# Two-layer decoder trunk: the next stage opens with token tile 0 alone, weights are split further ahead

## The chip, the cores and the metric

The kernel runs on one core of a Trainium2 chip. The metric is the device time of one execution in microseconds (us); lower is better. The engines are named as the profile names them: PE (TensorE matmul) and PEld (its weight loads), DVE (VectorE), ACT (ScalarE), POOL (GpSimd), SP (SyncE).

## The reference

Batch 1, 256 tokens, width 2048, two layers. All matrix products are in float32.

```python
h = x
for layer in range(2):
    if layer == 0: attn = moba_attention(h, w_qkv, w_o, rel_bias)   # 16 heads of 128; one block of 256 tokens: causal
    else:
        k, v = h @ w_kv                                              # 4 shared K/V heads
        attn = swa_attention(h, w_q, sinks, w_o, k, v, rel_bias)     # 16 query heads, window of 128, a sink per head
    h = layer_norm(ALPHA * h + attn, ln_g[layer, 0], ln_b[layer, 0])
    c = causal_conv_width_3(h @ w_up[layer]) + conv_b                # 2048 -> 2 x 5504
    g, v = split(c)
    ffn = (gelu(g) * v) @ w_down[layer]                              # 5504 -> 2048
    h = layer_norm(ALPHA * h + ffn, ln_g[layer, 1], ln_b[layer, 1])
```

## The kernel before, in words

**Numbers.** A float32 value is kept as the sum of a high part and a low part (`fp32r`). A product is three matmuls: high by high, high weight by low activation, low weight by high activation. The transposed activations lie in the tile `xT` as 16 blocks (`KB`) of 128 features; a block has 512 columns: the high parts of tokens 0 to 255, then their low parts. Token tile 0 is tokens 0 to 127, token tile 1 tokens 128 to 255.

**Weights.** All weights come as one stream of 724 pieces `[128, 1024]`, called halves. SP loads a half (512 KB) into one of four `raw` buffers. `split_upto(i)` emits, for each half up to number i, a copy of the high part by ACT (L86, `wh`) and the subtraction that leaves the low part by DVE (L87, `wl`), and then the load of a further half (L72). There are four places for split halves (`HALF_BUFS`). `take()` gives PE the next half after asking for splits three halves ahead (`AHEAD`). Every engine works through its own instructions in program order; the order is written by hand (`at`, `pe_at`: so many half-steps later).

**Stages.** Attention 0, feed-forward 0 (FFN 0), attention 1, feed-forward 1 (FFN 1). In an up-projection or a q or k projection, one unit (`ws_unit`) is 128 output features: two halves, 16 high-part weight blocks against all 512 columns (L229) and 16 low-part blocks against 256 (L232). In `project_out`, and for v, the weights move instead (L251 to L253): four chunks of 512 output columns, each with one accumulator for each token tile.

**Between stages.** The last 16 blocks (8 halves) of the last chunk of `project_out`, the window, are computed for token tile 0 first and then for token tile 1 (`tilewise`). So the layer norm of tile 0 runs while PE works on tile 1. To hold 8 halves, four of them lie in `xT`, which is idle then (`aside`, `SPARE`). After the norm (L322, L323, one pair for each of four column groups), `turn` transposes four blocks on PE (L332) and copies them into `xT` (ACT, L334), and `low` makes the low parts (DVE, L339). The norm of tile 1 can only start when PE has done the window. Before an FFN, the first unit runs 32 matmuls over the 256 high columns of both tiles (L213, L214), so each block waits for tile 1's turn; its 16 matmuls with the low columns follow (L218). Before attention 1, the v projection does its first 8 blocks for tile 0 alone.

**Pools.** Attention has its own pool (with `oT`, its output) and the FFN has its own (with `aT`, its activations); each opens when its stage begins.

Of the kernel before, what the change touches and what calls it, by code (L numbers as in the profile page):

```python
# [17 lines left out]
P = 128  # L18
# [11 lines left out]
WINDOW = 128  # L30
# [13 lines left out]
WINDOW_BLOCKS = 2 * (HALF_BUFS + SPARE)  # L44


@with_exitstack
def trunk(ctx: ExitStack, tc: tile.TileContext, wst, xT_in, x_in, relb, onehot, umask, sinks, conv_in, ln_g, ln_b, out):
# [13 lines left out]
    todo = {"load": 0, "split": 0}  # L62
# [12 lines left out]
    def split_upto(i):  # L75
        while todo["split"] <= min(i, n_halves - 1):
            s = todo["split"]
            r = raws.pop(s)
            if s in aside:
                j = aside.pop(s)  # L80
                wh, wl = (xT[:, k:k + 2, :].rearrange("p a b -> p (a b)") for k in (4 * j, 4 * j + 2))
            else:
                wh = spool.tile([P, HW], F32R, name="wh")
                wl = spool.tile([P, HW], F32R, name="wl")
            for c in pieces(s):
                nc.scalar.activation(wh[:, c], r[:, c], AF.Copy)  # L86
                nc.vector.tensor_tensor(out=wl[:, c], in0=r[:, c], in1=wh[:, c].bitcast(F32), op=ALU.subtract)  # L87
            halves[s] = (wh, wl)
            todo["split"] += 1
            load_weights()  # L90
# [24 lines left out]
    def take(ahead=AHEAD):  # L115
        i = nexth["i"]
        nexth["i"] += 1
        split_upto(i + ahead)
        run(before)
        return halves.pop(i)  # L120

    xT = big.tile([P, KB, 2 * T], F32R, name="xT")
    res = big.tile([P, 2, D], F32, name="res")

# [75 lines left out]
    def ws_unit(acc, feed=None):  # L200

        def cols(w, j):
            return w[:, j * P:(j + 1) * P]

        o = acc[:, 0:T]
        if feed:
            pair = [take(1 - i) for i in range(2)]
            for k in range(KB):  # L210
                feed(k)
                wh, wl = pair[k // 8]
                nc.tensor.matmul(o, cols(wh, k % 8), xT[:, k, 0:T], start=(k == 0), stop=False)  # L213
                nc.tensor.matmul(o, cols(wl, k % 8), xT[:, k, 0:T], start=False, stop=False)  # L214
            feed(KB)
            split_upto(nexth["i"] + AHEAD - 2)
            for k in range(KB):
                nc.tensor.matmul(o, cols(pair[k // 8][0], k % 8), xT[:, k, T:2 * T], start=False, stop=(k == KB - 1))  # L218
                if k % 8 == 7:
                    step()  # L220
                    split_upto(nexth["i"] + AHEAD - 2 + (k + 1) // 8)
                    if k < 8:
                        run(before)
            return
        for hf in range(2):
            wh, wl = take()
            for j in range(8):
                k = hf * 8 + j
                nc.tensor.matmul(acc, cols(wh, j), xT[:, k, :], start=(k == 0), stop=False)  # L229
            for j in range(8):  # L230
                k = hf * 8 + j
                nc.tensor.matmul(o, cols(wl, j), xT[:, k, 0:T], start=False, stop=(k == KB - 1))  # L232
            step()

    class Moving:
# [12 lines left out]
        def mm(self, acc, k, t, wh, wl):  # L248
            sh = self.src[:, k, t * P:(t + 1) * P]
            sl = self.src[:, k, T + t * P:T + (t + 1) * P]  # L250
# [20 lines left out]
        def chunk(self, accs, early=None, late=None):  # L271
# [3 lines left out]
            if early:  # L275
                k = 2 * HALF_BUFS
                self.tilewise(accs, 0, k, early)
# [14 lines left out]
    def project_out(src, nk, li, after, preload):  # L292
# [4 lines left out]
        aside.update({w0 + j: j for j in range(SPARE)})  # L297
# [44 lines left out]
        pts = {}  # L342

        def late(t, i):
            last = i == WINDOW_BLOCKS // 2 - 1
# [6 lines left out]
            if t == 1 and after and i >= SPARE:  # L352
                c = COLS[0][i - SPARE]
                pts[c] = turn(0, c)
                if not last:
                    low(0, c, pts[c])
                if i < SPARE + 2:
                    split_upto(w0 + WINDOW_BLOCKS // 2 + i - SPARE)
            if t == 1 and last:
                evac(NCH - 1, 1, accs[1])  # L360
                sd = moments(1)
                if after:
                    low(0, c, pts[c])
# [5 lines left out]
        for n in range(NCH):  # L369
            accs = [acc_tile(), acc_tile()]  # L370
            if n < NCH - 1:
# [71 lines left out]
    def layer_attention(l, rest):  # L443
        with tc.tile_pool(name=f"att{l}", bufs=2) as pool:
            oT = pool.tile([P, NH, 2 * T], F32R, name="oT", bufs=1)
            bias = pool.tile([P, NH, 2 * P], F32, name="bias", bufs=1)
            if l == 0:
                load_input(pool, lambda: bias_table(pool))
            else:
                nc.vector.tensor_scalar(nsk, sk, -1.0, None, op0=ALU.mult)  # L450
            for i, h in enumerate(range(0, NH, 4)):
                at(4 + (8 - 4 * l) * i, spread_bias, l, h, h + 4)
                at(4 + (8 - 4 * l) * i, load_bias, bias, l, h, h + 4)

            def v_group(early=None):
                mv = Moving(xT, KB)
                accs = [acc_tile(), acc_tile()]
                mv.chunk(accs, early=early)
                vt = pool.tile([P, 2, 512], F32, name="vt", bufs=1 if l else 2)

                def evac():
                    for t in range(2):
                        nc.scalar.activation(vt[:, t, :], accs[t], AF.Copy)

                at(0, evac)
                return vt

            def feat_unit(name, bufs):
                acc = acc_tile()
                ws_unit(acc)  # L470
                o = pool.tile([P, T], F32, name=name, bufs=bufs)

                def evac():
                    nc.scalar.activation(o, acc[:, T:2 * T], AF.Copy)
                    nc.vector.tensor_tensor(out=o, in0=acc[:, 0:T], in1=o, op=ALU.add)

                at(0, evac, first=True)
                return o

            if l == 0:  # L480
                for g in range(NH // 4):
                    vt = v_group()
                    for j in range(4):
                        h = 4 * g + j
                        q = feat_unit("qT", 4)
                        k = feat_unit("kT", 4)
                        attention(pool, l, h, q, vt[:, :, j * P:(j + 1) * P], k, bias, oT)
            else:
                norm, turned = rest
                for i, c in enumerate(COLS[0][:2]):  # L490
                    split_upto(nexth["i"] + 2 + i)
                    norm(c)

                def early(t, i):
                    if i == HALF_BUFS - 1:
                        turn, low = turned
                        pts = [(c, turn(c)) for c in (COLS[0][2:] if t else COLS[0][:2])]
                        for c, pt in pts:
                            low(c, pt)
                        if t == 0:  # L500
                            for c in COLS[0][2:]:
                                norm(c)
                    if t:
                        split_upto(nexth["i"] + i)

                vt = v_group(early)
                ks = [feat_unit("kT", KVH) for _ in range(KVH)]
                for h in range(NH):
                    q = feat_unit("qT", 4)
                    j = h // GRP  # L510
                    attention(pool, l, h, q, vt[:, :, j * P:(j + 1) * P], ks[j], bias, oT)
            return project_out(oT, NH, 2 * l, True, AF.Gelu_apprx_tanh)

    def layer_ffn(l, rest):
        with tc.tile_pool(name=f"ffn{l}", bufs=2) as pool:
            aT = pool.tile([P, FT, 2 * T], F32R, name="aT", bufs=1)
            cw = pool.tile([P, FT, 2, 4], F32, name="cw", bufs=1)
            nc.gpsimd.dma_start(cw, conv_in[l])
            norm, turned = rest
            turn, low = turned  # L520
            for c in COLS[1]:
                norm(c)
            pts = {}

            def feed(k):
                for b, c in zip(((0, 0),) + COLS[1], COLS[1]):
                    if k == b[0] and c not in pts:
                        pts[c] = turn(c)
                if k == KB:
                    for c in COLS[1]:  # L530
                        low(c, pts[c])

            def conv(i, s, acc, whole, c):
                w = cw[:, i, s, :]
                h = acc[:, 0:T]
                if not whole:
                    h = pool.tile([P, T], F32, name="h")
                    nc.scalar.activation(h, acc[:, T:2 * T], AF.Copy)
                    nc.vector.tensor_tensor(out=h, in0=acc[:, 0:T], in1=h, op=ALU.add)  # L539
# [115 lines left out]
```

## Time and profile before

| | us |
|---|---|
| median of 3 runs (2109.34 to 2110.36) | 2110.07 |
| the profiled execution | 2108.28 |
| its span, first to last instruction | 2106.2 |
| PE busy in the span | 2077.7 |
| DVE busy | 1434.3 |
| ACT busy | 989.6 |

The profile is one execution. A busy PE in it may still be a slow PE, because the ends of matmuls are modelled; the distance from one start to the next is what tells. The mean granted TensorE clock of the run is 0.996 of full speed.

### The profile page before, as it was taken

What the parts mean: (1) busy time and instruction counts of PE and PEld (TensorE: products, weight loads), DVE (VectorE), ACT (ScalarE), POOL (GpSimd) and SP (SyncE); (2) the same over time, 40 slices, a digit from 0 to 9 for tenths busy, and PEclk for the clock granted to TensorE, in tenths of its full rate; (3) what the DMA queues carried; (4) which work ended last, traced back from release to release, by engine and by line L of the source; (5) the groups of instructions that cost most, each with busy time, mean ns of one, the idle gap of its engine ahead of it and who ended that gap; (6) DMA issues with size and microseconds to landing.
All of it is one profiled execution on the core that took longest, in us unless ns stands there. A gap on an engine that the chain in (4) does not pass through costs nothing.

```text
span 2106.2 us, 28530 instructions
## 1 busy us (share of the span) xinstructions
PE 2077.7 (99%) x10972; PEld 1788.4 (85%) x10972; DVE 1434.3 (68%) x2104; ACT 989.6 (47%) x1395; POOL 23.5 (1%) x36
## 2 busy tenths in 40 slices
PE   9999999999999999999999999999999999999997
PEld 7888888788888888888887888888888888888886
DVE  5555555787787787754457676687787778764455
ACT  5454444355545455433344554455555554543342
POOL 0100000000000000000001000000000000000000
PEclk9999999999999999999999999999999999999999
DMA  8854546565555555556566544565555555555563
GB/s 279 293 191 170 178 163 204 180 207 189 187 188 189 190 190 188 185 190 198 193 207 214 212 146 159 180 214 190 190 189 183 191 187 189 190 189 191 193 196 130
DMA packets 114265, 405.08 MB, mean 192 GB/s; under 512 B 15649, under 2 KB 15969, under 8 KB 112849
## 3 DMA queue, kind: packets, MB, share of 16 engines
q1 hardware_dynamic: 106832, 383.67, 54.3%
q0 software_dynamic: 7008, 19.33, 2.6%
q8 instruction: 86, 1.41, 0.3%
q14 instruction: 51, 0.41, 0.1%
q10 hardware_dynamic: 288, 0.26, 0.0%
HBM read 401.02 MB, written 6.34 MB: 193 GB/s over the span
## 4 chain that ended last, share of the span: by engine, by line
PE 97%; DVE 2%; ACT 0%; issue 0%; DMA 0%; ACTq 0%; DVEq 0%
PE acc L229 39%; PE acc L232 20%; PE acc L252 12%; PE acc L251 12%; PE acc L253 12%; PE at L393 1%; PE at L426 1%; DVE wl L87 1%; PE at L419 0%; DVE res L322 0%; PE at L392 0%; PE at L427 0%; DVE res L323 0%; DVE xT L339 0%; PE at L332 0%
## 5 line engine op out<-in xcount | busy, mean ns | idle before, releaser
L87 DVE TENSOR_TENSOR wl<-raw,wh 128x1024 fp32r<-128x1024 f32 (+1 forms) x709 | 865.1, 1222 | 592.2 <-ACT wh L86 589.8
L86 ACT ACTIVATE wh<-raw 128x1024 fp32r<-128x1024 f32 (+1 forms) x709 | 750.3, 1059 | 901.0 <-PE acc L253 341.7
L229 PE MATMUL acc<-xT,wh 128*128 128x512 f32 x3552 | 896.3, 394 | 0.0
L229 PEld LDWEIGHTS acc<-xT,wh 128*128 128x128 f32 x3552 | 640.8, 189 | 116.0
L232 PEld LDWEIGHTS acc<-xT,wl 128*128 128x128 f32 x3552 | 484.5, 190 | 34.8
L232 PE MATMUL acc<-xT,wl 128*128 128x256 f32 x3552 | 495.2, 282 | 0.0
L251 PE MATMUL acc<-wh,aT 128*128 128x512 f32 x656 | 255.5, 389 | 0.0
L252 PE MATMUL acc<-wl,aT 128*128 128x512 f32 x656 | 255.2, 389 | 0.0
L253 PE MATMUL acc<-wh,aT 128*128 128x512 f32 x656 | 255.2, 389 | 0.0
L253 PEld LDWEIGHTS acc<-wh,aT 128*128 128x128 f32 x656 | 123.1, 188 | 25.6
L252 PEld LDWEIGHTS acc<-wl,aT 128*128 128x128 f32 x656 | 123.1, 188 | 25.5
L251 PEld LDWEIGHTS acc<-wh,aT 128*128 128x128 f32 x656 | 123.1, 188 | 25.4
L251 PE MATMUL acc<-wh,oT 128*128 128x512 f32 x224 | 88.9, 397 | 0.0
L253 PE MATMUL acc<-wh,oT 128*128 128x512 f32 x224 | 87.3, 390 | 0.0
L252 PE MATMUL acc<-wl,oT 128*128 128x512 f32 x224 | 87.3, 390 | 0.0
L541 DVE SCALAR_TENSOR_TENSOR c<-h,cw,c 128x255 f32<-128x255 f32 x170 | 82.2, 484 | 6.0
L542 DVE SCALAR_TENSOR_TENSOR c<-h,cw,c 128x254 f32<-128x254 f32 x170 | 82.2, 483 | 6.1
L540 DVE TENSOR_SCALAR c<-h,cw 128x256 f32<-128x256 f32 x170 | 70.1, 412 | 6.1
L539 DVE TENSOR_TENSOR h<-acc,h 128x256 f32<-128x256 f32 x170 | 70.8, 417 | 0.0
L251 PE MATMUL acc<-wh,xT 128*128 128x512 f32 x160 | 65.2, 408 | 4.8 <-ACT wh L86 4.6
L548 ACT ACTIVATE aT<-c 128x256 fp32r<-128x256 f32 x86 | 35.9, 418 | 69.8 <-DVE c L545 69.8
L252 PE MATMUL acc<-wl,xT 128*128 128x512 f32 x160 | 63.5, 397 | 1.7 <-DVE wl L87 1.7
(100 smaller groups left out, 1190.4 us busy)
## 6 DMA issues: line engine op xcount, KB each, us to landing
raw<-in_wst_dram SPq DMA_DIRECT2D x723, 512.0 KB, 3.4
band<-ud POOLq DMA_DIRECT2D x8, 512.0 KB, 14.3
bias<-band POOLq DMA_DIRECT2D x8, 512.0 KB, 5.7
gb<-in_ln_g_dram POOLq DMA_DIRECT2D x4, 1024.0 KB, 6.6
gb<-in_ln_b_dram POOLq DMA_DIRECT2D x4, 1024.0 KB, 9.3
res<-in_x_dram POOLq DMA_DIRECT2D x2, 1024.0 KB, 10.3
out_dram<-res SPq DMA_DIRECT2D x8, 256.0 KB, 2.5
xc<-in_xT_dram SPq DMA_DIRECT2D x7, 256.0 KB, 5.4
```

Source lines behind the costliest of these rows:

```text
L86: nc.scalar.activation(wh[:, c], r[:, c], AF.Copy)
L87: nc.vector.tensor_tensor(out=wl[:, c], in0=r[:, c], in1=wh[:, c].bitcast(F32), op=ALU.subtract)
L229: nc.tensor.matmul(acc, cols(wh, j), xT[:, k, :], start=(k == 0), stop=False)
L232: nc.tensor.matmul(o, cols(wl, j), xT[:, k, 0:T], start=False, stop=(k == KB - 1))
L251: nc.tensor.matmul(acc, sh, wh, start=(k == 0), stop=False)
L252: nc.tensor.matmul(acc, sh, wl, start=False, stop=False)
L253: nc.tensor.matmul(acc, sl, wh, start=False, stop=(k == self.nk - 1))
L539: nc.vector.tensor_tensor(out=h, in0=acc[:, 0:T], in1=h, op=ALU.add)
L540: nc.vector.tensor_scalar(c, h, w[:, 2:3], w[:, 3:4], op0=ALU.mult, op1=ALU.add)
L541: nc.vector.scalar_tensor_tensor(c[:, 1:T], h[:, 0:T - 1], w[:, 1:2], c[:, 1:T], op0=ALU.mult, op1=ALU.add)
L542: nc.vector.scalar_tensor_tensor(c[:, 2:T], h[:, 0:T - 2], w[:, 0:1], c[:, 2:T], op0=ALU.mult, op1=ALU.add)
L548: nc.scalar.activation(aT[:, i, 0:T], g, AF.Copy)
```

## The change

1. **Opening of an FFN.** `ws_opening` replaces the first four ordinary units: 16 high-part blocks of each of four units against the high and low columns of token tile 0 alone (a 2 by 128 pattern of columns, into the same pattern of the accumulator); then the same 64 blocks against tile 1, four blocks of each unit in turn, after the turn of those blocks; then the low parts of the four units as in an ordinary unit.
2. **Opening of attention 1.** The v projection does all 16 blocks for tile 0 and then all 16 for tile 1, before the attention pool opens.
3. **Splitting ahead.** High and low parts are counted apart (`high_upto`, `split_upto`). From the second chunk of a `project_out` on, split halves also lie in idle activations: before an FFN in `xT` (4), in `up` (6) and in the four old places, 14 in all; before attention 1 in `xT` and the four old places, 8, and for the window also in `st` and `up`. `reach` says how far `take` asks ahead. By the end of the window the first eight halves of the next stage have their high parts asked for, the first six also their low parts.
4. **Pools.** `st` is one constant tile for the attention output and the first 16 blocks of the FFN's activations; `up` holds the other 27 and opens after the first chunk of the attention's `project_out` (`turnover`), with the load of `cw`. The pool of attention 1 opens after its v projection, so its bias loads start there.
5. The turns of tile 0 in the window come one half earlier. Line numbers move: L87 is L99 in the changed kernel, L86 L92, L332 L384, L229 L232, L232 L235.

```diff
+    def ws_opening(accs, between, done):
+        n0 = nexth["i"]
+        nexth["i"] += 2 * len(accs)
+        run(before)
+        pair = [[halves.pop(n0 + 2 * u + i) for i in range(2)] for u in range(len(accs))]
+        def high(u, t, ks):
+            part = lambda a: a.rearrange("p (s t c) -> p s t c", s=2, t=2)[:, :, t, :]
+            for k in ks:
+                nc.tensor.matmul(part(accs[u]), cols(pair[u][k // 8][0], k % 8), part(xT[:, k, :]),
+                                 start=(t == 0 and k == 0), stop=False)
+        for u in range(len(accs)):
+            between(u)
+            high(u, 0, range(KB))
+        for c in range(KB // 4):
+            between(len(accs) + c)
+            for u in range(len(accs)):
+                high(u, 1, range(4 * c, 4 * c + 4))
+        for u, acc in enumerate(accs):
+            for k in range(KB):
+                nc.tensor.matmul(acc[:, 0:T], cols(pair[u][k // 8][1], k % 8), xT[:, k, 0:T],
+                                 start=False, stop=(k == KB - 1))
...
+        def settle():
+            ring, h = homes()
+            aside.update({w0 - len(ring) + j: x for j, x in enumerate(ring) if x})
+            aside.update({w0 + SPARE + j: h[j] for j in range(4)})
+            aside.update({n0 + 4: h[4], n0 + 5: h[5], n0 + 6: h[0], n0 + 7: h[1]})
+            first = w0 - len(ring) - AHEAD
+            for i in range(first, w0 + 3):
+                reach[i] = i + min(AHEAD + (i - first) * 3 // 5, len(ring) - 1)
+            for i, s in enumerate((4, 6, 7, 9, 11, 12, 13), w0 - 4):
+                reach[i] = min(max(reach[i], w0 + s), n0 + 5)
...
-            if t == 1 and after and i >= SPARE:
-                c = COLS[0][i - SPARE]
-                pts[c] = turn(0, c)
...
+            if t == 1 and after:
+                if 3 <= i < 7:
+                    c = COLS[0][i - 3]
+                    low(0, c, turn(0, c))
+                if 5 <= i < 7:
+                    high_upto(n0 + i + 1)
...
+            for c in cc[:3]:
                 norm(c)
+            def between(i):
+                if i == OPENING - 1:
+                    low(cc[0], turn(cc[0]))
+                    norm(cc[3])
+                if OPENING <= i < OPENING + 3:
+                    c = cc[i - OPENING + 1]
+                    low(c, turn(c))
+                    if i > OPENING:
+                        split_upto(n0 + i + 1)
```

In these names `w0` is the first half of the window and `n0` the first half of the next stage.

**PE at the start of FFN 0, before:** `at<-ident,res` is a transpose, `acc<-xT,wh` a matmul with a high part of weights, `acc<-xT,wl` with a low part.

```order
L253 MATMUL acc<-wh,oT 128x512
L332 MATMUL at<-ident,res 128x128 x12
L213 MATMUL acc<-xT,wh 128x256
L214 MATMUL acc<-xT,wl 128x256
L213 MATMUL acc<-xT,wh 128x256
L214 MATMUL acc<-xT,wl 128x256
```

**PE at the same place, with the change** (`up` holds split weights here):

```order
L287 MATMUL acc<-up,st 128x512
L250 MATMUL acc<-xT,wh 128x2x128 x32
L250 MATMUL acc<-xT,up 128x2x128 x16
L384 MATMUL at<-ident,res 128x128 x4
L250 MATMUL acc<-xT,up 128x2x128 x16
L384 MATMUL at<-ident,res 128x128 x4
L250 MATMUL acc<-xT,wh 128x2x128 x8
L250 MATMUL acc<-xT,up 128x2x128 x8
L384 MATMUL at<-ident,res 128x128 x4
```

Before, two turns of tile 1 stand right behind the window (behind the last turn of tile 0); with the change, 48 matmuls of tile 0 stand ahead of the first turn of tile 1, and 16 matmuls ahead of each further one.

**DVE at the same place, with the change:** L358 and L359 take the last accumulator into the residual, L363 and L411 give the moments, L374 and L375 are the norm, L391 is `low`, L99 the split, L617 to L620 the convolution.

```order
L411 RECIPROCAL rs<-sd 128x1
L374 SCALAR_TENSOR_TENSOR res<-res,ag,gb 128x512
L375 SCALAR_TENSOR_TENSOR res<-res,rs,gb 128x512
L374 SCALAR_TENSOR_TENSOR res<-res,ag,gb 128x512
L375 SCALAR_TENSOR_TENSOR res<-res,rs,gb 128x512
L374 SCALAR_TENSOR_TENSOR res<-res,ag,gb 128x512
L375 SCALAR_TENSOR_TENSOR res<-res,rs,gb 128x512
L391 TENSOR_TENSOR xT<-at,xT 128x4x128
L374 SCALAR_TENSOR_TENSOR res<-res,ag,gb 128x512
L375 SCALAR_TENSOR_TENSOR res<-res,rs,gb 128x512
L391 TENSOR_TENSOR xT<-at,xT 128x4x128 x2
L99 TENSOR_TENSOR up<-raw,up 128x1024
```

Before, the four norm pairs stand together, then four `low`, then four splits; now the first `low` stands behind the third pair, and only two of the eight opening halves are still to be split behind the norm.

## Rows read from the trace of the kernel before

**Rows 1.** The page: the span, and PE in part 1.

```profile
span 2106.2 us, 28530 instructions
PE 2077.7 (99%) x10972; PEld 1788.4 (85%) x10972; DVE 1434.3 (68%) x2104; ACT 989.6 (47%) x1395; POOL 23.5 (1%) x36
```

**Rows 2.** Waits of PE over the run: us in total, times, longest.

```profile
PE at L332 <- DVE res L323: 5.1, 3, 3.6
PE acc L251 <- ACT wh L86: 4.6, 2, 3.1
PE at L332 <- issue: 3.6, 1, 3.6
```

**Rows 3.** Timeline of PE around the start of FFN 0: start, us, instruction.

```profile
385.57 0.60 PE L332 MATMUL at<-ident,res 128*128 128x128 f32 x4
385.93 0.48 PE L251 MATMUL acc<-wh,oT 128*128 128x512 f32 x1
386.25 0.40 PE L252 MATMUL acc<-wl,oT 128*128 128x512 f32 x1
...
391.06 0.60 PE L332 MATMUL at<-ident,res 128*128 128x128 f32 x4
395.21 0.63 PE L332 MATMUL at<-ident,res 128*128 128x128 f32 x4 [3.55 <-issue]
...
405.30 2.00 PE L229 MATMUL acc<-xT,wh 128*128 128x512 f32 x8
```

**Rows 4.** A window behind that wait; the third number from the end is PEclk.

```profile
396.60:400.00 3.40, 3.29 (x17) 3.32 (x17) 3.33 (x6) 0.60 (x1) 0.24 (x1) 0.50 0.00 0
```

**Rows 5.** Timeline of PE at the start of FFN 1.

```profile
1371.71 0.60 PE L332 MATMUL at<-ident,res 128*128 128x128 f32 x4
...
1385.45 1.78 PE L229 MATMUL acc<-xT,wh 128*128 128x512 f32 x7
```

**Rows 6.** Timeline of PE at the start of attention 1.

```profile
1115.52 0.60 PE L332 MATMUL at<-ident,res 128*128 128x128 f32 x4
...
1120.36 0.50 PE L251 MATMUL acc<-wh,xT 128*128 128x512 f32 x1 [1.47 <-ACT wh L86]
...
1144.88 1.98 PE L229 MATMUL acc<-xT,wh 128*128 128x512 f32 x8
```

**Rows 7.** Timeline of PE inside an up-projection.

```profile
700.44 1.12 PE L232 MATMUL acc<-xT,wl 128*128 128x256 f32 x8
701.39 2.00 PE L229 MATMUL acc<-xT,wh 128*128 128x512 f32 x8
703.23 1.11 PE L232 MATMUL acc<-xT,wl 128*128 128x256 f32 x8
```

**Rows 8.** Timeline of DVE behind the window of attention 0.

```profile
391.36 0.68 DVE L306 SCALAR_TENSOR_TENSOR res<-res,acc 128x512 f32<-128x512 f32 x1
...
393.59 0.73 DVE L322 SCALAR_TENSOR_TENSOR res<-res,ag,gb 128x512 f32<-128x512 f32 x1
...
395.03 0.75 DVE L322 SCALAR_TENSOR_TENSOR res<-res,ag,gb 128x512 f32<-128x512 f32 x1
```

**Rows 9.** The page, part 5: the two splits of a half; us busy, mean ns.

```profile
L87 DVE TENSOR_TENSOR wl<-raw,wh 128x1024 fp32r<-128x1024 f32 (+1 forms) x709 | 865.1, 1222 | 592.2 <-ACT wh L86 589.8
L86 ACT ACTIVATE wh<-raw 128x1024 fp32r<-128x1024 f32 (+1 forms) x709 | 750.3, 1059 | 901.0 <-PE acc L253 341.7
```

**Rows 10.** Loads at L72, issue to landing: windows 420:700, then 404:409.

```profile
DMA to landing us min/median/max: 3.0/3.3/4.6
...
DMA to landing us min/median/max: 6.9/8.9/9.5
```

**Rows 11.** A window in attention 1; last two numbers: DMA share, GB/s.

```profile
1156.00:1167.00 11.00, 11.00 (x65) 9.66 (x64) 5.57 (x6) 4.63 (x7) 0.00 (x0) 1.00 1.01 419
```

**Rows 12.** Timeline of DVE in an up-projection: first and fifth instruction of a convolution.

```profile
702.92 0.42 DVE L539 TENSOR_TENSOR h<-acc,h 128x256 f32<-128x256 f32 x1
...
704.86 0.42 DVE L545 TENSOR_TENSOR c<-c,c 128x256 f32<-128x256 f32 x1
```

More of the change, by code (lines that the diff above doesn't have):

```diff
@@ L29 @@
 MAXD = 128
-WINDOW = 128
+SWA = 128
 ALPHA = math.sqrt(2.0)
@@ L61, in trunk @@
     raws, halves, aside = {}, {}, {}
-    todo = {"load": 0, "split": 0}
+    todo = {"load": 0, "high": 0, "low": 0}
+    reach, placed = {}, {}
     def pieces(u):
@@ L84, in split_upto, with low_piece @@
                 wl = spool.tile([P, HW], F32R, name="wl")
+            halves[s] = placed[s] = (wh, wl)
             for c in pieces(s):
[L86 to L89, printed above, removed]
+                nc.scalar.activation(wh[:, c], raws[s][:, c], AF.Copy)
+                if len(pieces(s)) > 1:
+                    low_piece(s, c)
+            todo["high"] += 1
+    def low_piece(s, c):
+        wh, wl = placed[s]
+        nc.vector.tensor_tensor(out=wl[:, c], in0=raws[s][:, c], in1=wh[:, c].bitcast(F32), op=ALU.subtract)
+    def split_upto(i):
+        while todo["low"] <= min(i, n_halves - 1):
+            s = todo["low"]
+            high_upto(s)
+            if len(pieces(s)) == 1:
+                low_piece(s, slice(0, HW))
+            raws.pop(s), placed.pop(s)
+            todo["low"] += 1
             load_weights()
@@ L198, in load_bias, with cols, ws_unit @@
         nc.gpsimd.dma_start(bias[:, h0:h1, :], band[l, h0:h1].rearrange("h q j -> q h j"))
-    def ws_unit(acc, feed=None):
-        def cols(w, j):
-            return w[:, j * P:(j + 1) * P]
+    def cols(w, j):
+        return w[:, j * P:(j + 1) * P]
+    def ws_unit(acc):
         o = acc[:, 0:T]
[L208 to L224, printed above, removed]
         for hf in range(2):
@@ L370, in project_out @@
             accs = [acc_tile(), acc_tile()]
+            if n == 1 and turnover:
+                turnover()
+            if n == 1 and after:
+                settle()
             if n < NCH - 1:
@@ L441, in attention @@
         at(5, outputs)
[L443 to L512, printed above, removed]
@@ new lines, in trunk, with __init__, __call__, homes @@
+    class FeedForward:
+        def __init__(self, l, stage):
+            self.l, self.stage = l, stage
+        def __call__(self):
+            self.pool = pool = self.stage(f"ffn{self.l}")
+            self.up = pool.tile([P, FT - NH, 2 * T], F32R, name="up", bufs=1)
+            self.cw = pool.tile([P, FT, 2, 4], F32, name="cw", bufs=1)
+            nc.gpsimd.dma_start(self.cw, conv_in[self.l])
+        def homes(self):
+            x, h = ([(tile, j) for j in range(n)] for tile, n in ((xT, SPARE), (self.up, 6)))
+            return x + h[:4] + HALF_BUFS * [None] + h[4:], h
+        def block(self, k):
+            return st[:, k, :] if k < NH else self.up[:, k - NH, :]
+        def run(self, rest):
+            l, pool = self.l, self.pool
+            norm, (turn, low) = rest
+            n0 = nexth["i"]
+            cc = COLS[1]
+            for c in cc[:3]:
+                norm(c)
+            def between(i):
[7 more added lines that the diff above has]
+                        split_upto(n0 + i + 1)
+            def conv(i, s, acc, c):
+                w = self.cw[:, i, s, :]
+                h = pool.tile([P, T], F32, name="h")
+                nc.scalar.activation(h, acc[:, T:2 * T], AF.Copy)
+                nc.vector.tensor_tensor(out=h, in0=acc[:, 0:T], in1=h, op=ALU.add)
@@ L547, in store @@
             def store(i, g):
-                nc.scalar.activation(aT[:, i, 0:T], g, AF.Copy)
-                nc.vector.tensor_tensor(out=aT[:, i, T:2 * T], in0=g, in1=aT[:, i, 0:T].bitcast(F32), op=ALU.subtract)
-            for i in range(FT):
-                g, v = (pool.tile([P, T], F32, name=f"c{s}") for s in range(2))
-                for s, c in enumerate((g, v)):
-                    first = i == 0 and s == 0
-                    acc = acc_tile()
-                    ws_unit(acc, feed if first else None)
-                    at(0, conv, i, s, acc, first, c)
-                    if s == 0:
-                        at(1, nc.scalar.activation, c, c, AF.Gelu_apprx_tanh)
-                at(0, gate, i, g, v)
-                at(1, store, i, g)
@@ L562, in layer_ffn, with after @@
-            return project_out(aT, FT, 2 * l + 1, l == 0, AF.Exp)
-    rest = None
-    for l in range(2):
-        rest = layer_ffn(l, layer_attention(l, rest))
+                b = self.block(i)
+                nc.scalar.activation(b[:, 0:T], g, AF.Copy)
+                nc.vector.tensor_tensor(out=b[:, T:2 * T], in0=g, in1=b[:, 0:T].bitcast(F32), op=ALU.subtract)
+            cs = {}
+            def after(u, acc):
+                i, s = divmod(u, 2)
+                cs[s] = pool.tile([P, T], F32, name=f"c{s}")
+                at(0, conv, i, s, acc, cs[s])
+                if s == 0:
+                    at(1, nc.scalar.activation, cs[0], cs[0], AF.Gelu_apprx_tanh)
+                else:
+                    at(0, gate, i, cs[0], cs[1])
+                    at(1, store, i, cs[0])
@@ new lines, in run, with opened @@
+            accs = [acc_tile() for _ in range(OPENING)]
+            def opened(u):
+                after(u, accs[u])
+                if u < 2:
+                    split_upto(n0 + 2 * OPENING + 2 * u + 1)
+            ws_opening(accs, between, opened)
+            for u in range(OPENING, 2 * FT):
+                acc = acc_tile()
+                ws_unit(acc)
+                after(u, acc)
+            homes = None
+            if l == 0:
+                x, h = ([(tile, j) for j in range(n)] for tile, n in ((xT, SPARE), (st, 4)))
+                homes = lambda: (x + HALF_BUFS * [None], h + [(self.up, j) for j in range(2)])
@@ L569, in _bucket, with stage @@
+            return project_out(self.block, FT, 2 * l + 1, homes, AF.Exp)
+    with ExitStack() as held:
+        def stage(name):
+            held.close()
+            return held.enter_context(tc.tile_pool(name=name, bufs=2))
+        rest = None
+        for l in range(2):
+            ff = FeedForward(l, stage)
+            rest = ff.run(layer_attention(l, rest, stage, ff))
 def _bucket(d):
```

136 lines of the change are left out of this document (94 added, 42 removed).

## The prediction, as put on record before the changed kernel ran

> **What bounds the kernel now.** I read the page first. PE is busy for 2077.7 of 2106.2 us [rows 1], so only time in which PE stands still or runs slowly can be won, unless matmuls are taken out, and the change takes none out. Then the list of PE's waits: the three that matter are at the transposes L332 and at L251 [rows 2]. Last the timelines of PE at the three stage changes, where all of them lie.
>
> At the start of FFN 0 PE issues the last turn of token tile 0 at 391.06, then nothing of tile 1 until 395.21, and the first ordinary unit starts at 405.30 [rows 3]. What lies in these 14.24 us has a price. A turn is four transposes; at 385.57 it takes 0.36 to the next matmul, and that one 0.32 to the one after (386.25) where 0.23 is usual [rows 3]; so 0.45 a turn, and five turns 2.25. A 256-column matmul takes 0.119 from start to start (eight between 700.44 and 701.39) [rows 7]; the first unit has 48, so 5.7. Together 8.0: **6.2 us are lost.** [...] At FFN 1 the same stretch is 1371.71 to 1385.45, 13.74 [rows 5], **5.8 lost**. At attention 1, 1115.52 to 1144.88 is 29.36 [rows 6]; it holds five turns (2.25) and 96 matmuls of 512 columns at 0.227 (the distance of those in this chain; 1.84/8 = 0.23 in a unit [rows 7]), 21.8; **5.3 lost**, the first of it 1.47 on a split by ACT [rows 6]. In all 17.3 us.
>
> What is late at the FFNs is the norm of tile 1. The last accumulator is read by DVE 0.3 behind the window's end (391.36 against 391.06), the norm starts 2.2 later (393.59), and each column group takes 1.44 (to 395.03) [rows 8]. So the first group is ready 4.0 us behind the end of the window, the others at 5.4, 6.9 and 8.3, and PE has only tile 0's last turn to do meanwhile.
>
> **The change, part by part.**
>
> *Opening of an FFN.* I count from E, the end of the window. PE now has three units of tile 0 before it comes to a turn of tile 1: 48 matmuls, 5.7 us. The first group is normed at 4.0, so that turn does not wait. Then 16 more matmuls (1.9) to the next turn, at 8.1; its group is ready at 5.4. DVE makes the first low part behind the third norm pair, at 7.6; PE needs it at about 8.6. The third turn is at 10.4 and the last at 12.8; the fourth norm pair ends by 9.1. Behind each turn ACT and DVE need about 0.7 each (a turn's copy and its low part have 512 columns, as the evacuation of 0.68 in [rows 8]); the columns turned at 10.4 are needed at 12.8, one turn and 16 matmuls later. So each step has 1 us or more in hand, and I take the wait and the low clock as gone. The price: the first unit had 48 matmuls of 256 columns already; three further units now have 48 (5.71) where an ordinary one takes 2 x 2.79 = 5.58 (700.44 to 703.23 is one half) [rows 7]. That is 0.4 a stage. The transposes are as many. So FFN 0 gains 6.2 - 0.4 = 5.8 and FFN 1 gains 5.4.
>
> That the opening matmuls go at 0.119 isn't shown: their columns are two runs of 128, in `xT` and in the accumulator. From below, nothing extra: L232 loads a new weight block for every 256 columns too and keeps 0.119 [rows 7]. From above, the 0.23 of a 512-column matmul: 256 of them (64 in each of two passes, two stages), 28 us. I take the lower end: the same number of columns goes through, and L232 is the same instruction but for the runs. [...]
>
> *Opening of attention 1.* Tile 0 now has 16 blocks, 48 matmuls, 10.9 us, instead of 8. The first two turns stand at 8.2, the norms of these groups end at 4.0 and 5.4; then DVE splits two halves (1.22 each [rows 9], to 7.9) and norms the third group (9.3). The low parts come at 10 and 12, tile 1 starts near 11.9 and needs the second group 2.7 later. The count of matmuls and turns is the same. Gain 5.3.
>
> *Halves for the openings.* An FFN opening needs 8 halves split early, attention's too. Supply: a load takes 3.3 from issue to landing when little else is in flight [rows 10], then ACT 1.06 and DVE 1.22 [rows 9]; with four `raw` buffers that is one half in (3.3 + 1.06 + 1.22)/4 = 1.4 us. The engines moved 419 GB/s in one stretch in which PE never stood still [rows 11], 1.25 us for 512 KB, so bandwidth allows it. Demand: before an FFN the lead grows over the 17 halves ahead of the window, 2.72 each (12 matmuls of 0.227), in which 27 halves are to be split: 46/27 = 1.7 us each. Before attention 1, 21 halves in 11 x 2.72 + 2 x 1.36 = 32.6: 1.55. Both are slower than 1.4. And the last of them has until the end of tile 0's pass, 8 us later, before it holds up DVE's norm of tile 0. Cost nothing; if this cover is gone, see the second rival.
>
> *What queues behind it.* Splits stand in the same queues as the norm: on DVE a split that waits for its load holds the evacuation behind it, and through it tile 0's turns. That bites only when the last split of the lead comes over 8 us late. Loads: SP issues one behind each low part, in order; two of them (n0 + 10, n0 + 11) now go out only behind the two late splits, at about 13.5 and 16, and are needed at 30. POOL's queue keeps its order; `cw` is loaded a stage part earlier, and the bias loads of attention 1 some 22 us later, with 4 k units and a q unit (10 x 2.79 = 28 us) before the first is read. I cost these at nothing.
>
> *Behind the FFN opening* four convolutions come within 7.7 us instead of one per 5.6. On DVE a convolution is 1.94 (702.92 to 704.86) [rows 12], so four and four splits are 12.7 us from about 18 on: finished near 31, with the next half (n0 + 12) needed at 35.9. Nothing, with some 3 us in hand.
>
> Attention heads, units, the chunks, the start and the tail behind the last window stay as they are.
>
> **Sum.** 5.8 + 5.4 + 5.3 = 16.5 us. I take 0.5 off for waits of a few tenths such as [rows 6] have around turns: 16.0. Against the profiled execution: 2108.28 (2106.2 span and 2.1 around it) becomes 2092.3. The median of the three runs is 1.8 above that execution, so the median becomes 2110.07 - 16.0 = **2094 us**.
>
> **Rivals.**
>
> 1. *As summed.* 2091 to 2097: all three losses gone but for 0 to 3.5 us.
> 2. *Supply is late.* In favour: at the start of FFN 0 four loads took 6.9 to 9.5 instead of 3.3 [rows 10], and DVE works through norms, splits and convolutions in one queue. With 8.9 for a load, a half would take (8.9 + 2.3)/4 = 2.8 instead of 1.4, as slow as PE uses them. A lead that is short by two or three halves at E makes PE wait 1.4 to 2.8 each. Against: before the windows little else is loaded. Two stages with 4 us: 2094 + 8 = 2102; range 2097 to 2105.
> 3. *It doesn't do what it says.* The lead isn't built, because the places come free too late; then PE waits at E for the halves that it lacks, about as long as for the norm now: 5 us a stage, 2107 to 2110. Against: `xT` and `up` are idle by then.
> 4. *Slower: opening matmuls with split columns go at half the rate.* 256 x 0.11 = 28 us, 2094 + 28 = 2122. It decides from 16/256 = 0.063 us extra each, a start-to-start distance over 0.18. For it: no row shows the pattern. Against: runs of 512 bytes, and as many columns. [...]
>
> **How the numbers follow.** I give the first 0.70, the second 0.17, the third 0.05, the fourth 0.08. Within 0.2% of 2110 (about what a measurement tells from no change) is 2105.9 to 2114.3: only the third falls there. So faster 0.87, same 0.05, slower 0.08. The forecast is 2094; the range reaches up into the second case, 2091 to 2102, and leaves out its tail and the last two, together under 0.2.
>
> **What would show it.** Right: no wait of PE over 0.5 us at the three stage changes, the granted clock at 1.00 through both FFN openings, and 24.7 us from E to the fifth unit (four turns and 192 matmuls). Matmuls of the opening 0.119 apart; 0.23 would show the fourth. Waits of PE on `wh` or `wl` behind the window would show the second, with loads over 6 us ahead of it. I am wrong if a turn of tile 1 still waits for the norm, or if DVE's tile-0 norm starts late because a split ahead of it waits for its load.

## The result and the profile after

The changed kernel takes **2092.33 us** (median of 4 runs, 2091.68 to 2092.53); the kernel before took 2109.7 beside it. The ratio is 0.9919, 95% interval 0.9907 to 0.9931: 17.4 us less, where 16.0 were forecast. The profiled execution took 2091.68.

The page of the changed kernel, its span and the engines' busy times, answers to [rows 1]:

```profile
span 2089.6 us, 28703 instructions
PE 2074.0 (99%) x11068; PEld 1791.7 (86%) x11068; DVE 1437.0 (69%) x2106; ACT 988.8 (47%) x1397; POOL 23.5 (1%) x36
```

PE's waits over the whole run, the answer to [rows 2]:

```profile
PE acc L285 <- ACT wh L92: 2.5, 1, 2.5
PE at L186 <- POOL ident masks.py:199: 1.4, 1, 1.4
```

These are all; both lie in the first 10 us. No wait is listed at a stage change any more. PE stands still for 15.6 of its span, 28.5 before: 12.9 of the 16.6 us by which the span is shorter. The other 3.7 are busy time that is gone although there are 96 matmuls more; the stretch of [rows 4], 3.4 us at a granted clock of 0.50 where it is 1.00 now, is part of it. The windows over the three stage changes (PEclk is the third number from the end) and over the stretch of [rows 4]:

```profile
380.00:405.00 25.00, 25.00 (x175) 23.08 (x174) 19.39 (x31) 8.53 (x14) 2.17 (x3) 1.00 0.13 44
1105.00:1140.00 35.00, 35.00 (x174) 29.31 (x174) 22.01 (x30) 15.38 (x21) 1.90 (x2) 1.00 0.38 118
1360.00:1386.00 26.00, 26.00 (x215) 25.79 (x214) 19.85 (x28) 10.25 (x16) 1.05 (x2) 1.00 0.45 165
396.60:400.00 3.40, 3.40 (x32) 3.40 (x31) 3.08 (x5) 0.67 (x2) 0.00 (x0) 1.00 0.00 0
```

PE's timeline at the places of [rows 3], [rows 6] and [rows 5]: the opening of FFN 0 up to its fifth unit (L262 are the low parts of the opening), the first unit behind the v projection of attention 1, the fifth unit of FFN 1.

```profile
391.18 4.00 PE L250 MATMUL acc<-xT,wh 128*128 128x256 f32 x32
395.02 2.08 PE L250 MATMUL acc<-xT,up 128*128 128x256 f32 x16
396.94 0.60 PE L384 MATMUL at<-ident,res 128*128 128x128 f32 x4
397.30 2.16 PE L250 MATMUL acc<-xT,up 128*128 128x256 f32 x16
...
408.27 4.00 PE L262 MATMUL acc<-xT,wl 128*128 128x256 f32 x32
412.11 4.00 PE L262 MATMUL acc<-xT,up 128*128 128x256 f32 x32
415.95 2.00 PE L232 MATMUL acc<-xT,wh 128*128 128x512 f32 x8
...
1133.56 1.98 PE L232 MATMUL acc<-xT,wh 128*128 128x512 f32 x8
...
1385.64 2.00 PE L232 MATMUL acc<-xT,wh 128*128 128x512 f32 x8
```

These rows say how much each stage change gave. An FFN's first ordinary unit stood behind one opening unit before, now behind four; three ordinary units are 3 x 2 x 2.79 = 16.74. So FFN 0 compares 405.30 + 16.74 = 422.04 [rows 3] with 415.95: 6.09 earlier. Attention 1 compares 1144.88 [rows 6] with 1133.56: 11.32 earlier. FFN 1 compares 1385.45 + 16.74 = 1402.19 [rows 5] with 1385.64: 16.55 earlier, and the span is 16.6 shorter, so nothing is given back behind it. Of the 6.09, 0.4 is older: the first unit of the run starts at 31.38 instead of 31.77, behind a first wait for ACT of 2.5 that was 3.1 [rows 2]. That is luck and not the change: in open1, open3 and ring8 below, which start as the changed kernel does, this wait is 3.4, 3.2 and 2.4. That leaves **5.7 for FFN 0, 5.2 for attention 1, 5.2 for FFN 1 and 0.4 at the start.**

DVE's timeline around the window of attention 0; the bracket is the idle time ahead of an instruction and what ended it.

```profile
372.20 2.34 DVE L99 TENSOR_TENSOR up<-raw,up 128x1024 fp32r<-128x1024 f32 x2
378.62 0.69 DVE L358 SCALAR_TENSOR_TENSOR res<-res,acc 128x512 f32<-128x512 f32 x1 [4.08 <-PE acc L287]
...
381.58 0.75 DVE L375 SCALAR_TENSOR_TENSOR res<-res,rs,gb 128x512 f32<-128x512 f32 x1
...
393.54 0.73 DVE L374 SCALAR_TENSOR_TENSOR res<-res,ag,gb 128x512 f32<-128x512 f32 x1
```

The reader is to see two things. Tile 1's norm is as late as it was (393.54 here, 393.59 in [rows 8]): nothing became faster, PE only has other work meanwhile. And DVE, done with the lead, stood idle for 4.08 us before tile 0's last accumulator came: the lead had 4.1 us in hand. The number matters below.

### The profile page after: what moved, and what is told of

Read it like the earlier page. It is cut to its first block, busy times and chain, and to the rows that moved or that the text cites. A ratio compares the mean times of both kernels' runs of the same rounds, so it can differ in the third digit from the quotient of the medians.

```text
span 2089.6 us, 28703 instructions
## 1 busy us (share of the span) xinstructions
PE 2074.0 (99%) x11068; PEld 1791.7 (86%) x11068; DVE 1437.0 (69%) x2106; ACT 988.8 (47%) x1397; POOL 23.5 (1%) x36
## 4 chain that ended last, share of the span: by engine, by line
PE 99%; DVE 0%; DMA 0%; ACT 0%; ACTq 0%; issue 0%
PE acc L232 38%; PE acc L235 20%; PE acc L285 12%; PE acc L286 12%; PE acc L287 12%; PE acc L250 1%; PE acc L262 1%; PE at L444 1%; PE at L477 1%; PE at L470 1%; PE at L384 1%; PE at L443 0%; PE at L478 0%; DMA xc<-in_xT_dram 0%; DVE res L375 0%; DVE res L374 0%
## 5 line engine op out<-in xcount | busy, mean ns | idle before, releaser
L99 DVE TENSOR_TENSOR wl<-raw,wh 128x1024 fp32r<-128x1024 f32 (+1 forms) x663 | 809.6, 1222 | 553.9 <-ACT wh L92 546.6
L92 ACT ACTIVATE wh<-raw 128x1024 fp32r<-128x1024 f32 (+1 forms) x663 | 701.5, 1059 | 820.7 <-PE acc L287 277.1
L232 PE MATMUL acc<-xT,wh 128*128 128x512 f32 x3456 | 872.3, 394 | 0.0
L232 PEld LDWEIGHTS acc<-xT,wh 128*128 128x128 f32 x3456 | 623.5, 189 | 112.9
L235 PEld LDWEIGHTS acc<-xT,wl 128*128 128x128 f32 x3456 | 471.4, 190 | 33.9
L235 PE MATMUL acc<-xT,wl 128*128 128x256 f32 x3456 | 481.8, 282 | 0.0
L285 PE MATMUL acc<-wh,up 128*128 128x512 f32 x378 | 147.0, 389 | 0.0
L286 PE MATMUL acc<-wl,up 128*128 128x512 f32 x378 | 147.0, 389 | 0.0
L287 PE MATMUL acc<-wh,up 128*128 128x512 f32 x378 | 147.0, 389 | 0.0
L285 PE MATMUL acc<-wh,st 128*128 128x512 f32 x366 | 143.6, 392 | 0.0
L287 PE MATMUL acc<-wh,st 128*128 128x512 f32 x366 | 142.5, 389 | 0.0
L286 PE MATMUL acc<-wl,st 128*128 128x512 f32 x366 | 142.4, 389 | 0.0
L620 DVE SCALAR_TENSOR_TENSOR c<-h,cw,c 128x254 f32<-128x254 f32 x172 | 83.2, 484 | 6.2
L287 PEld LDWEIGHTS acc<-wh,up 128*128 128x128 f32 x378 | 71.0, 188 | 14.8
L285 PEld LDWEIGHTS acc<-wh,up 128*128 128x128 f32 x378 | 71.0, 188 | 14.7
L286 PEld LDWEIGHTS acc<-wl,up 128*128 128x128 f32 x378 | 71.0, 188 | 14.6
L287 PEld LDWEIGHTS acc<-wh,st 128*128 128x128 f32 x366 | 68.7, 188 | 14.6
L285 PEld LDWEIGHTS acc<-wh,st 128*128 128x128 f32 x366 | 68.7, 188 | 13.9
L286 PEld LDWEIGHTS acc<-wl,st 128*128 128x128 f32 x366 | 68.8, 188 | 13.8
L617 DVE TENSOR_TENSOR h<-acc,h 128x256 f32<-128x256 f32 x172 | 71.8, 418 | 1.5 <-ACT h L616 1.5
```

Source lines behind the costliest of these rows:

```text
L92: nc.scalar.activation(wh[:, c], raws[s][:, c], AF.Copy)
L99: nc.vector.tensor_tensor(out=wl[:, c], in0=raws[s][:, c], in1=wh[:, c].bitcast(F32), op=ALU.subtract)
L285: nc.tensor.matmul(acc, sh, wh, start=(k == 0), stop=False)
L286: nc.tensor.matmul(acc, sh, wl, start=False, stop=False)
L287: nc.tensor.matmul(acc, sl, wh, start=False, stop=(k == self.nk - 1))
L620: nc.vector.scalar_tensor_tensor(c[:, 2:T], h[:, 0:T - 2], w[:, 0:1], c[:, 2:T], op0=ALU.mult, op1=ALU.add)
```

## The experiments

Two questions: is it the length of tile 0's work that hides the norm (the cover), and what does the cover need from the splits that run ahead (the lead)? The kernel before ran beside each experiment, with medians of 2109.6 to 2110.2 us; each ratio is against the one beside it.

**The cover, in four doses.** `OPENING` is the number of units that open an FFN with tile 0. All of them but one, 16 matmuls or 1.92 us each, stand ahead of tile 1's first turn.

```diff
-OPENING = 4
+OPENING = 3    # open3; 2 in open2, 1 in open1
```

open3: 

> Opening of three units instead of four in both FFNs. Cover theory (PE needs enough tile-0 matmuls to outlast the norm of tile 1): two units last 3.8 us, the first column group is normed 4.0 us behind the window, so the first turn waits about 0.25, and the low parts come late by 0.2 to 0.8 at three of four steps: about 1.5 us a stage, 3 us slower than the changed kernel in all, about 2095. Rival (the halves split ahead did it, the length of the opening does not matter): within 0.5 us of the changed kernel, 2092.

open2: 

> Opening of two units. Cover theory: one unit lasts 1.9 us, the first turn waits 2.1, the low parts make the other steps late by 0.7 to 0.8 each: about 4.4 us a stage, less 0.3 of split units; 8 us slower than the changed kernel, about 2100. PE never stands still long at one stretch, so the granted clock stays at 1.00. Rival (halves split ahead did it): 2092.

open1: 

> Opening of one unit, all else as in the changed kernel, so the first turn of tile 1 again stands right behind the window. Cover theory: the turn waits 4.0, two more low parts are late by about 1 each: 7 us a stage, and the granted clock falls to 0.50 for some 3.4 us behind the wait as it did before the change, 1.7 more; 14 to 17 us slower than the changed kernel, 2106 to 2109, of the two FFN gains nothing is left. Rival (halves split ahead did it): 2092 to 2094.

| | median us | ratio, 95% interval | cover ahead of the turn | PE's wait at the turn, each FFN |
|---|---|---|---|---|
| as changed (4) | 2092.33 | 0.9919, 0.9907 to 0.9931 | 5.76 | none |
| open3 | 2094.71 | 0.9923, 0.9906 to 0.9939 | 3.84 | none listed; 0.5 and 0.4 behind it |
| open2 | 2100.53 | 0.9951, 0.9936 to 0.9966 | 1.92 | 1.9 |
| open1 | 2106.02 | 0.9981, 0.9972 to 0.9991 | 0 | 3.9 and 3.8 |

PE at the window's end and at the first turn of tile 1 in open3, FFN 0:

```profile
392.30 4.00 PE L250 MATMUL acc<-xT,wh 128*128 128x256 f32 x32
396.28 0.63 PE L384 MATMUL at<-ident,res 128*128 128x128 f32 x4
```

PE's waits of open1, where the cover is gone:

```profile
PE at L384 <- DVE res L375: 3.9, 1, 3.9
PE at L384 <- issue: 3.8, 1, 3.8
...
PE acc L250 <- DVE xT L391: 1.5, 3, 0.7
```

In open3, open2 and open1 the first turn of tile 1 starts 3.97 to 4.02 us behind the window's end, in both FFNs, as a norm that is ready at 4.0 asks: in open1 and open2 PE waits for it, and in open3 it is 0.14 and 0.18 late (3.98 and 4.02 instead of 3.84), too little for the list. What open3 loses lies behind that turn, where only 12 matmuls stand between two turns and PE waits for the low part L391: from the window's end to the first ordinary unit, with one ordinary unit (5.58) added, it takes 25.9 in each FFN against 24.77. The forecasts of the time came true in open3 and open2, and in open1 at their lower edge. In open1 4.2 us of the gain are left (1.9 to 5.9 by the interval), which leaves room for the 5.2 of attention 1 and for nothing else.

In open2 the clock was a miss. PE's timeline at FFN 0 and at FFN 1, and the window behind the first wait:

```profile
395.23 0.63 PE L384 MATMUL at<-ident,res 128*128 128x128 f32 x4 [1.90 <-issue]
395.62 3.37 PE L250 MATMUL acc<-xT,wh 128*128 128x256 f32 x16
398.79 0.96 PE L384 MATMUL at<-ident,res 128*128 128x128 f32 x4
...
1369.25 0.63 PE L384 MATMUL at<-ident,res 128*128 128x128 f32 x4 [1.95 <-DVE res L375]
1369.64 2.16 PE L250 MATMUL acc<-xT,wh 128*128 128x256 f32 x16
1371.63 0.60 PE L384 MATMUL at<-ident,res 128*128 128x128 f32 x4
```

```profile
396.10:399.50 3.40, 3.40 (x19) 3.40 (x18) 3.33 (x6) 0.39 (x1) 0.00 (x0) 0.50 0.00 0
```

Behind the first wait the same 16 matmuls take 398.79 - 395.62 = 3.17 to the next turn, most of it at half the clock; behind the second 1.99. The waits are alike.

**Attention 1 alone undone.** v8 goes back to 8 blocks of v for tile 0, 8 for tile 1, then both together.

```diff
-                k = WINDOW_BLOCKS
+                k = 2 * HALF_BUFS
...
-                if t == 0 and i == 5:
-                    pts = [turn(c[j]) for j in range(2)]
...
+                if i == HALF_BUFS - 1:
+                    pair = c[2:4] if t else c[0:2]
+                    pts = [turn(x) for x in pair]
```

> Only the opening of attention 1 is undone: the v projection does 8 blocks for tile 0, 8 for tile 1, then both; the halves are split ahead as in the changed kernel, and the two late splits stand behind the first low parts. Two parts theory (at attention 1 the lead takes most of the 5.3 us, the longer tile-0 pass the rest): PE waits about 1.1 for the first low part of tile 1 and 1.3 for the third, 2.4 in all: 2094 to 2096. Rival (the longer pass alone took the 5.3): 2097 to 2098. Rival (the lead alone): 2092.

Measured 2097.2, ratio 0.994 (0.9925 to 0.9954). PE waits there again, as its list shows:

```profile
PE acc L285 <- ACT xT L386: 1.7, 2, 1.4
...
PE acc L287 <- DVE xT L391: 0.6, 1, 0.6
```

The window's end, the first unit behind the v projection, and the clock behind those waits:

```profile
1110.82 0.39 PE L285 MATMUL acc<-wh,xT 128*128 128x512 f32 x1
...
1139.41 1.98 PE L232 MATMUL acc<-xT,wh 128*128 128x512 f32 x8
```

```profile
1128.20:1131.60 3.40, 3.40 (x10) 2.62 (x10) 1.51 (x3) 0.16 (x1) 0.00 (x0) 0.56 0.94 320
```

It stands 4.9 over the changed kernel, and so does the stretch: 28.59 (1110.82 to 1139.41) against 23.68 (1109.88 to 1133.56). That was the time of the first rival (the longer pass alone), not of the two-parts theory. The theory's waits came, 2.3 where 2.4 were expected; it had left out the low clock behind them, 0.56 for 3.4 us, which costs 1.5; the other 1.1 stands in no list. So nearly all of the 5.2 hangs on the longer pass: in these timelines the early splits without it keep 0.3.

**The lead undone: order, places, both.** nolead keeps the places in idle activations, but asks early only for the halves of the opening, in the window; ring4 keeps the order in which splits are asked for, but gives them four places ahead of the window; neither does both.

```diff
 nolead:
-            for i in range(first, w0 + 3):
-                reach[i] = i + min(AHEAD + (i - first) * 3 // 5, len(ring) - 1)
-            for i, s in enumerate((4, 6, 7, 9, 11, 12, 13), w0 - 4):
-                reach[i] = min(max(reach[i], w0 + s), n0 + 5)
+            for i, s in enumerate((11, 12, 13), w0):
+                reach[i] = w0 + s
 ring4, in attention and in the FFN:
-            return x + h[:4] + HALF_BUFS * [None] + h[4:], h
+            return HALF_BUFS * [None], h
...
-                homes = lambda: (x + HALF_BUFS * [None], h + [(self.up, j) for j in range(2)])
+                homes = lambda: (HALF_BUFS * [None], h + [(self.up, j) for j in range(2)])
```

nolead: 

> Splits run three halves ahead until the window begins, and only there are asked for up to the sixth half of the next stage; openings as in the changed kernel. Lead theory: from the window's start some 10 halves at 1.4 us and two evacuations of 2.7 us stand on DVE ahead of the norm of tile 0, which starts up to 6 us late; PE waits at the turns of tile 0, 4 to 6 us at each of three stage changes: 2104 to 2110. Rival (supply of 1.4 us a half is fast enough without a lead): under 1 us a stage, 2092 to 2095.

ring4: 

> The splits keep their early places in the program, but ahead of the window there are only the four old places (no ring of 14 or 8); the window's own halves still go into idle activations. Order theory (what counts is that few splits stand on DVE between the last evacuation ahead of the window and the norm of tile 0; the idle places of the window itself let the engines run ahead): at the attention stages the last splits come some 3 us late, 1.5 of it in hand, so 1 to 2 us a stage, none at attention 1: 2094 to 2096. Rival (the 14 places make the lead): 4 us or more at each of three stage changes, over 2104.

neither: 

> No places ahead of the window and no early splits, openings as in the changed kernel. Order theory: as without the early splits alone, 2111 to 2113, with waits of nearly 8 us at the turns of tile 0 in both attention stages and still none at the start of attention 1. Rival (the places carried the start of attention 1 there): a wait of 3 us or more at attention 1 too, 2115 or more.

| | median us | ratio, 95% interval | PE's waits for tile 0's norm |
|---|---|---|---|
| nolead | 2111.83 | 1.0009, 0.9999 to 1.0018 | 15.4 in 2, at the FFNs |
| ring4 | 2107.27 | 0.9989, 0.9979 to 0.9998 | 11.0 in 3 |
| neither | 2116.94 | 1.0033, 1.0019 to 1.0047 | 19.2 in 3 |

With the order gone, the whole gain is gone; with the places gone, all but 2.6 us (0.4 to 4.4 by the interval); without both the kernel is slower than before. nolead was a miss: its time lies above the 2104 to 2110 expected, with waits of nearly 8 at two changes instead of 4 to 6 at three. In the run without both the rival came true. The theory for ring4 (that the order alone counts) fell. DVE's timeline in ring4 before FFN 0 shows how:

```profile
367.34 4.81 DVE L99 TENSOR_TENSOR up<-raw,up 128x1024 fp32r<-128x1024 f32 x4 [2.57 <-ACT up L92]
...
383.66 0.68 DVE L358 SCALAR_TENSOR_TENSOR res<-res,acc 128x512 f32<-128x512 f32 x1
...
386.61 0.75 DVE L375 SCALAR_TENSOR_TENSOR res<-res,rs,gb 128x512 f32<-128x512 f32 x1
```

And PE's, with the first turn of tile 0:

```profile
387.42 0.66 PE L384 MATMUL at<-ident,res 128*128 128x128 f32 x4 [3.50 <-DVE res L375]
```

The splits run late, the evacuation L358 stands behind them without any idle time ahead of it (383.66 instead of 378.62), and through the norm (386.61 + 0.75 = 387.36) it holds up the turn. So a late lead is not felt as a wait for weights, as the second rival had it, but as a wait for the norm of tile 0. In nolead it is the same, with the evacuation at 388.33 and waits of 7.6 and 7.8; but it has no wait at attention 1: DVE runs ahead by itself there, as far as there are places, and stands idle for 2.20 before tile 0's evacuation. Without the places PE waits there too, 2.96 in ring4 and 3.14 in the run neither. So attention 1 needs the longer pass and the places, but not the early order.

**How many places, how many loads.** ring8 gives attention's lead 8 places instead of 14 (the six in `up` are left out). raw3 has three `raw` buffers instead of four.

```diff
 ring8:
-            return x + h[:4] + HALF_BUFS * [None] + h[4:], h
+            return x + HALF_BUFS * [None], h
 raw3:
-RAW_BUFS = 4
+RAW_BUFS = 3
```

raw3: 

> Three raw buffers instead of four, nothing else. If the supply of the lead is set by loads in flight (load 4.6 plus ACT 1.06 and DVE 1.22, divided by the buffers), a half takes 2.3 instead of 1.7 us, the lead of about 10 halves comes out some 6 us late or three halves short, and PE waits at all three stage changes: 2 to 6 us each, 2098 to 2108 us, with the low clock behind some of the waits. If a load gets shorter when fewer are in flight (the bandwidth is the limit, 1.25 us for a half), three do what four did: no wait of PE over 0.5 us at a stage change, 2092 to 2093.5 us. At the old estimate (load 3.3) a half would take 1.9 us, later than 1.7 but inside the 4 us that DVE had in hand: also 2092 to 2094.

ring8: 

> The attention stages' lead has 8 places instead of 14 (xT and the four old places; up is not used ahead of the window). If the places are needed in proportion to the lead that the first ones hold (no place ahead of the window cost 15 us over three stage changes), four of ten places more give back most of it: 0 to 2 us of PE's wait at each of the two changes to an FFN, none at attention 1, 2092 to 2096 us. The rival: the lead only works with all 14, a wait of 3 us or more and the low clock at each change to an FFN, 2099 to 2103 us.

ring8 takes 2092.13, ratio 0.992 (0.9903 to 0.9936): as fast as the changed kernel, at the lower edge of its first theory, no wait of PE at a stage change. What the six places are worth is seen in DVE's timeline:

```profile
375.16 2.35 DVE L99 TENSOR_TENSOR up<-raw,up 128x1024 fp32r<-128x1024 f32 x2
377.99 0.69 DVE L358 SCALAR_TENSOR_TENSOR res<-res,acc 128x512 f32<-128x512 f32 x1 [0.48 <-PE acc L287]
```

0.48 us in hand instead of 4.08: time to spare, and no time of the kernel.

raw3 takes 2117.54, ratio 1.004 (1.0025 to 1.0055): slower than before, and far above what was expected. First the loads of the lead before FFN 0 in the changed kernel (count, first and last issue; who waited for them, in us and times; min, median and max from issue to landing), then those of raw3:

```profile
L75 SPq DMA_DIRECT2D raw<-in_wst_dram x24: 327/328/328, 328.8 to 369.7; - x24
...
  ACT up L92: 6.5, 9
  ACT wh L92: 5.6, 8
  ACT xT L92: 2.1, 3
...
DMA to landing us min/median/max: 3.3/4.7/5.9
```

```profile
L75 SPq DMA_DIRECT2D raw<-in_wst_dram x18: 327/328/328, 336.2 to 374.2; - x18
...
DMA to landing us min/median/max: 3.3/4.3/5.3
```

Raw3's 18 loads are (374.2 - 336.2)/17 = 2.24 apart, those of the changed kernel (369.7 - 328.8)/23 = 1.78. That is the 2.3 of the first theory: with three buffers a load lands hardly sooner than with four (4.3 against 4.7), so the number of buffers and the time that one is taken set the supply. In the changed kernel too ACT waited for a load ahead of 20 of the 24 splits, so there it is the loads that set the pace and not the program. Its waits, and its tile 0 evacuation:

```profile
PE at L384 <- DVE res L375: 15.5, 3, 5.9
...
PE at L443 <- DVE kT L553: 1.0, 1, 1.0
PE at L477 <- ACT PT L473: 0.6, 1, 0.6
PE at L443 <- DVE qT L553: 0.2, 1, 0.2
```

```profile
388.30 0.68 DVE L358 SCALAR_TENSOR_TENSOR res<-res,acc 128x512 f32<-128x512 f32 x1
```

The miss was in the time. 15.5 us of waits at the three changes, the low clock behind each (0.69 from 391.8 to 398.6, 0.68 from 1118.6 to 1125.4, 0.57 from 1376.6 to 1383.4: 2.1, 2.2 and 2.9 us) and 1.8 of new waits in attention make 24.5 of the 25.9 by which its profiled execution stands over the changed kernel's. The theory had the supply and the waits right (5.3, 5.9 and 4.4, where 2 to 6 each were expected); its time left out that the low clock follows all three, and the waits in attention.

## Why the prediction was right, point by point

- **What bounds it.** Right: but for 0.4 at the start, the gain lies at the three stage changes. With less cover (open3, open2, open1) tile 1's turn stands where the 4.0 us of the norm put it.
- **The terms of the sum.** Forecast 5.8, 5.3 and 5.4, measured 5.7, 5.2 and 5.2 in the profiled execution. The sum was 16.5 less 0.5; measured 16.2, and 0.4 at the start that was not forecast. So the terms were 0.1 to 0.2 too high each, and the 0.5 for small waits was not needed; these errors go against each other. The profiled execution gained 16.6, the medians 17.4; the interval (14.6 to 19.6 of 2109.7) doesn't tell these apart. The pools and the earlier turns of tile 0 were not undone by themselves; they were forecast at nothing, and that they give nothing of their own is not shown.
- **The price of the split columns.** From the window's end to the fifth unit 24.7 was forecast; 391.18 to 415.95 is 24.77. 32 of the opening's matmuls take 395.02 - 391.18 = 3.84, 0.120 each, against 0.119 assumed and 0.23 at the upper end; 32 of its low parts, whose columns are one run of 256, take the same 3.84 (408.27 to 412.11). The fourth rival is out: here two runs of 128 columns cost what one run of 256 does. That they might cost more was an estimate, with the 0.23 of a 512-column matmul [rows 7] as its upper end.
- **The supply: mis-sized.** "One half in 1.4 us" was made from a load of 3.3 [rows 10], measured where little is in flight. In the lead, with all four buffers in use, it is 4.7: (4.7 + 1.06 + 1.22)/4 = 1.75, and the demand before an FFN was 1.7. So supply was no faster than demand. The 8 us that the last of the lead was to have in hand came out as 4.1. The forecast held because of that reserve, not because supply was ahead: raw3 shows the other side, where 0.46 us more a half (2.24 against 1.78) over 27 halves is 12 us, more than the reserve (tile 0's evacuation came at 388.30 instead of 378.62, 9.7 late with the 4.1 used up).
- **The second rival** was dearer than its 8 us: where the lead is late, PE waits 3.0 to 5.9 us a stage in ring4 and raw3 and up to 8.5 in the run neither, with a low clock (0.50 to 0.60 over 3.4 us) behind five of the six waits of ring4 and raw3, and the kernel ends at 2107 to 2118. Its sign was misread too: I looked for waits on `wh` or `wl`, but the wait is on tile 0's norm, as the prediction's last sentence named. (The 8 us stood for two stages of 4; it is late at three in ring4 and raw3.)
- **Behind the FFN opening, SP's order, the pools:** costed at nothing, and no wait of PE stands there.
- **The low clock** of [rows 4], 0.50 behind a wait of 3.55, stood behind most of the waits at a turn, not behind all (below): over 3.4 us behind the turn it was 0.50 at both of nolead, at all three of raw3 and at one of open2's two, 0.60 and 0.50 at two of ring4's three. In the changed kernel, with no such wait, the clock stays at 1.00 through the three stage changes, as forecast.

## What to carry to other kernels

A wait for a norm on the path of PE can be covered by independent work of the same stage, and the cover that the first step needs is read from the trace as one number (here 4.0 us). The steps behind need theirs too: open3 covered the first but for 0.2 us and still lost 1.1 us a stage. More units than four were not tried. Such a cover moves the demand for weights forward, so work out the supply from the round trip of a load at the number of loads in flight that the lead will have, not from a quiet stretch (here 4.7 us against 3.3). When weight splits run ahead in the queue of the engine that also evacuates results, and come late, the evacuation pays for it (here 383.66 in ring4 instead of 378.62): read what that engine has in hand before its next critical instruction.

## What the runs showed of the hardware that was not expected

- The clock didn't follow the length of PE's wait. It fell to 0.50 behind a wait of 1.90 at FFN 0 of open2 (16 matmuls in 3.17), and behind 1.95 at FFN 1 of the same run 16 matmuls took 1.99. Before the change it fell to 0.50 behind 3.55 [rows 4]; in ring4 it stayed at 1.00 from 387.4 to 394.2, behind 3.50. The executions of one program differ as well: those of the kernel before, beside the experiments, took 2107.3 to 2108.5 at a mean granted clock of 0.997 and 2109.2 to 2112.6 at 0.995 (2108.2 to 2111.6 at 0.996), and one of v8's four took 2094.9 at 0.998, the others 2097.0 to 2097.5 at 0.997. That the clock falls behind a wait in some executions and not in others fits this, but no trace here shows two executions of one kernel. What decides it was not settled.
- A 512 KB load of the lead before FFN 0 took 4.3 us from issue to landing (median) with three `raw` buffers and 4.7 with four, against 3.3 in a quiet stretch of the kernel before [rows 10].
